# Weight tiles loaded through ScalarE's queue, and softmax weights turned on VectorE and through DRAM instead of on TensorE

## The chip, the cores and the metric

The kernel runs on one core of one Trainium2 chip. The metric is the device time of the whole program in microseconds (us), as a median over several executions. One execution was taken with the hardware profiler; every time that is read from a profile belongs to that execution.

Five engines work side by side: TensorE (PE in the profile, with its weight loads as PEld), VectorE (DVE), ScalarE (ACT), GpSimd (POOL) and SyncE (SP), which here only issues transfers. A transfer (DMA) is issued from the instruction stream of one engine and then runs by itself.

## The reference

One step of a decoder layer for a prompt of 1024 tokens and, with the same weights, for a sample group of 8 sequences of one token. One combined projection of the normalised input feeds three branches: gated linear attention (GLA), multi-scale pooling, and attention to 256 memory tokens ("cross"). Cut to what matters here:

```
h = rmsnorm(x, norm_gain)
proj = h @ w_in                          # 1024 x 10256
q, k, v, gla_g, a_lr, u, pool_g, xq, xg, merge = split(proj)
...
def cross_attn(q, mk, mv):               # 4 heads of 256, 256 memory tokens
    s = einsum('bthd,bmhd->bhtm', q, mk) * (XA_HEAD_DIM ** -0.5)
    p = softmax(s, axis=-1)
    return einsum('bhtm,bmhd->bthd', p, mv)
c = cross_attn(xq, mem_k, mem_v)         # the sample rows have a memory of their own, one per sequence
br_x = c * silu(xg)
...
merged = sum(sigmoid(merge) * (branches @ w_branch))
y = rmsnorm(x + merged @ w_out)
```

All of it is fp32.

## The kernel before

**Precision.** A large product is made of three: each operand is split into a high part (a copy in TensorE's fast fp32r type, on ScalarE) and a low part (the rest, by a subtraction on VectorE). `split`, `split_r`, `split_in` do that, `mm3` is the three matmuls (lines 242 to 244: high x high, high x low, low x high).

**The input projection** runs as 40 `Pair`s, each of 256 columns of `w_in`. `load` brings the weights of a pair as two halves of 512 KB ("raw", a pool of three buffers). A pair is computed by seven products instead of eight (a Strassen-Winograd scheme), whose left operands are a11, a12, s2, s1, s3, s4 and a22, made of quarters of the raw tiles and their sums (`operands`). `seq` is the list of all products in order, `prepare` makes operands up to three products ahead of TensorE, and `run_product` runs one: 24 matmuls for each of two halves of the columns (one half of 258 columns per `yield`). In `prepare` stand the raw loads too: the high half of pair i+1 at product 4 of pair i, the low half of pair i+2 at product 6 of pair i. Both are issued by SyncE.

**Everything else is filled in between.** The cross stage, then GLA, then pooling are written as generators that yield after each small step, and `fill` runs such steps between the halves of products, according to a budget of work. So TensorE's and SyncE's instruction order is that in which the code is written (`manual_schedule`); on VectorE, ScalarE and GpSimd a scheduler of the language sets the order.

**The cross stage** (`cross_steps`, some 119 to 380 us) goes through 16 units, a unit being one of four heads and one of four chunks of 256 tokens. For a unit: `cross_fetch` and `cross_queries` load and split the queries; `cross_scores` makes scores (12 matmuls), the maximum, the exponential and the scaled softmax weights `p`, with tokens on the partitions; `cross_weights` turns `p` (four transposes on TensorE into one bank of PSUM) and splits it to `pT`, with memory positions on the partitions; `cross_values` multiplies `pT` with the memory's values (12 matmuls), copies the result out and writes it to DRAM. Step s of the loop does scores of unit s, values of unit s-2 and weights of unit s-1.

Between them runs a second chain, `cross_sample`, once for each head, for the sample rows, whose memory is another one for each sequence: `cross_rows` turns the eight queries and GpSimd writes them to DRAM (`xqs`); SyncE loads them back, two at a time and spread over all partitions (`qb`), with two blocks of keys (`kc`), in four rounds; VectorE multiplies and sums (L777); TensorE turns the sums `sc` (L791), then the softmax weights `ps` (L803), then multiplies with the values `vc` (L817). The tiles `kc`, `qb` and `vc` share a pool of four buffers (`V`).

Most other tiles of the stage (`xq`, its high part, `p`, `pT`, its parts, `xo`) come from one ring of 14 buffers (`R`, NR). PSUM has six banks for the projection (`PX`) and two for the stage (`PZ`).

GLA already has the detour that the change uses: `gla_out` transposes in blocks of 32 x 32 on VectorE (`go`, L992) and sends the blocks to their places in DRAM by four transfers on GpSimd (`onsc`, L994).

Of the kernel before, what the change touches and what calls it, by code (L numbers as in the profile page):

```python
# [18 lines left out]
P = 128  # L19
# [5 lines left out]
NH = 4  # L25
# [8 lines left out]
CT = 256  # L34
# [13 lines left out]
def trunk_kernel(ctx: ExitStack, tc: tile.TileContext,  # L48
# [3 lines left out]
    nc = tc.nc  # L52
# [46 lines left out]
    def PZ():  # L99
        return ps.tile([P, 512], F32, tag="pz", name="pz", bufs=2)  # L100
# [36 lines left out]
    ident = cp.tile([P, P], F32, name="ident")  # L137
# [67 lines left out]
    xq_scr, v_scr = scratch(NH, "xqs", (NS, 256)), scratch(NH, "vs", (NS, 256))  # L205
    acc_scr = [scratch(NK, f"acc{n}_", (P, TT)) for n in range(2)]
    mkv_scr = [scratch(NH, f"mkvs{o}", (P, 2, DV)) for o in range(2)]
    al_scr = scratch(2, "als", (P, HT))
# [9 lines left out]
    last = {}  # L218
# [10 lines left out]
    def split_r(src, shape, name, scale=None):  # L229
        hi, lo = R(shape, F32R, name + "h"), R(shape, F32R, name + "l")  # L230
        split(hi, lo, src, scale)
        return hi, lo

    def split_in(x, shape, name, scale=None):

        hi, lo = R(shape, F32R, name + "h"), x.bitcast(F32R)
        split(hi, lo, x, scale)
        return hi, lo

    def mm3(out, lh, ll, rh, rl, start, stop, more=False):  # L240

        nc.tensor.matmul(out, lhsT=lh, rhs=rh, start=start, stop=False, skip_group_check=more)  # L242
        nc.tensor.matmul(out, lhsT=lh, rhs=rl, start=False, stop=False, skip_group_check=more)  # L243
        nc.tensor.matmul(out, lhsT=ll, rhs=rh, start=False, stop=stop, skip_group_check=more)  # L244
# [42 lines left out]
    class Pair:  # L287
# [3 lines left out]
            self.src, self.dst, self.s0, self.gated, self.raw = src, dst, s0, gated, [None, None]  # L291
            self.turned = turned

        def load(self, i):
            raw = RAW("raw")
            nc.sync.dma_start(out=raw, in_=self.src.rearrange("(k p) n -> p k n", p=P)[:, 4 * i:4 * i + 4])
            self.raw[i] = raw

        def operands(self):
# [26 lines left out]
    pairs = []  # L326
# [8 lines left out]
    NPAIR = len(pairs)  # L335
# [12 lines left out]
    def prepare(n):  # L348

        while prep["n"] < min(n + 1, len(seq)):  # L350
            i, j = seq[prep["n"]]
            p = pairs[i]
            if j == 0:
                p.gen = p.operands()
            left[i, j] = next(p.gen)

            if (i, j) == (0, 1):
                pairs[1].load(0)
            if j == 4 and i + 1 < NPAIR:
                pairs[i + 1].load(1)  # L360
            elif j == 6 and i + 2 < NPAIR:
                pairs[i + 2].load(0)
            prep["n"] += 1


# [334 lines left out]
    def cross_scores(h, c):  # L700
        xh, xl = cross["q", h, c]
        mh, ml = cross["mk", h]
        t = PZ()
        for j in range(2):
            for i in range(2):
                cs = slice(j * P, (j + 1) * P)
                mm3(t[:, j * NM:(j + 1) * NM], xh[:, i, cs], xl[:, i, cs], mh[:, i], ml[:, i], i == 0, i == 1)
        nm = tiny(2, "nm")
        nc.vector.tensor_reduce(nm, t.rearrange("p (j m) -> p j m", j=2), axis=AX.X, op=ALU.max, negate=True)
        p = R([2, NM], name="p")  # L710
        sm = tiny(2, "sm")
        for j in range(2):
            act(p[:, j], t[:, j * NM:(j + 1) * NM], AF.Exp, bias=nm[:, j:j + 1], accum_out=sm[:, j:j + 1])
        nc.vector.reciprocal(sm, sm)
        for j in range(2):
            nc.vector.tensor_scalar(p[:, j], p[:, j], sm[:, j:j + 1], None, op0=ALU.mult)
        cross["p", h, c] = p

    def cross_weights(h, c):
        p = cross["p", h, c]  # L720
        t = PZ()
        for a in range(2):
            for j in range(2):
                nc.tensor.transpose(t[:, (2 * a + j) * P:(2 * a + j + 1) * P], p[:, j, a * P:(a + 1) * P], ident)
        cross["pT", h, c] = split_r(t.rearrange("p (a t) -> p a t", a=2), [2, CT], "pT")

    def cross_values(h, c):
        ph, pl_ = cross["pT", h, c]
        vh, vl = cross["mv", h]
        g = R([2, CT], name="xo")  # L730
        t = PZ()
        for i in range(2):
            cs = slice(i * P, (i + 1) * P)
            for a in range(2):
                mm3(t[:, i * CT:(i + 1) * CT], vh[:, a, cs], vl[:, a, cs], ph[:, a], pl_[:, a], a == 0, a == 1)
        nc.scalar.activation(g, t.rearrange("p (i t) -> p i t", i=2), AF.Copy)
        nc.gpsimd.dma_start(out=mix_chunk(2, h, c), in_=g)

# [93 lines left out]
    def cross_steps():  # L832
        def scores(n):
            cross_scores(n // 4, n % 4)

        def memory(n):
            if n % 4 == 0:
                cross_memory(n // 4)

        def weights(n):  # L840
            cross_weights(n // 4, n % 4)

        def values(n):
            cross_values(n // 4, n % 4)

        samples = chain_of(cross_sample(h) for h in range(NH))
        cross_load(0)
        cross_memory(0)
        cross_fetch(0, 0)
        yield 2  # L850
        cross_queries(0, 0)
        cross_fetch(0, 1)
        for s in range(16 + 2):
            if s < 16:
                scores(s)
                yield 3
                if s + 1 < 16:
                    cross_queries(*divmod(s + 1, 4))
                if s + 2 < 16:
                    cross_fetch(*divmod(s + 2, 4))  # L860
            if s % 4 == 2 and s < 14:
                cross_load(s // 4 + 1)
            if s >= 1:
                yield next(samples, 0)
            if 0 <= s - 2:
                values(s - 2)
                yield 1.7
# [404 lines left out]
    for tb in range(4):  # L1272
        load_x(tb)
    next(memory)
    pairs[0].load(0)
    for tb in range(4, 8):
        load_x(tb)
    pairs[0].load(1)

    mem_transposed()  # L1280
    next(memory)
# [196 lines left out]
    for hf, order in enumerate(ORDERS):  # L1478
        for tb in order:
# [23 lines left out]
            n, a = hf, 0  # L1503
# [62 lines left out]
```

## Time and profile before

| | |
|---|---|
| median of 3 executions | 1443.5 us (1441.85 to 1443.95) |
| the profiled execution | 1445.01 us, of which the span of instructions 1443.3 |
| TensorE's granted clock, mean | 0.997 |
| busy: PE / DVE / ACT / POOL | 98% / 63% / 47% / 15% |
| moved by transfers | 259.42 MB, 180 GB/s |

How to read it: "busy" is the share of the span in which an engine executed instructions. A row of waits names the engine and line that waited, and behind `<-` the engine, the tile and the line that ended last before it could go on. Matmuls are pipelined, so a matmul's own duration (0.28 us) is longer than the distance between two starts (0.12 us); the distance is what it costs. In names of operations, `pz<-ident,p` is: out, then in. Line numbers are those of the kernel before; behind the change the same code stands one to six lines lower.

### The profile page before, as it was taken

The page shows a single profiled execution, that of the slowest core. Times are in us where ns is not written, and L with a number is a line of the kernel's source. Part 1 is how long each engine was busy: PE and PEld are TensorE (multiplying, and loading weights), DVE is VectorE, ACT ScalarE, POOL GpSimd, SP SyncE. Part 2 cuts the span into 40 slices and gives each one's busy share as a digit, 9 for nine tenths or more (in the row PEclk, how much of TensorE's full clock was granted, in tenths as well). Part 3 has the DMA queues.
Part 4 walks back from the last instruction along what each step waited for, and adds up shares of the span by engine and source line. Part 5 has one row for each costly group of instructions (what it writes and reads, how often), then busy time and mean ns, then how long its engine had stood idle before and what let it go on. Part 6 is the DMA issues. An engine that isn't in the chain of part 4 may idle for free.

```text
span 1443.3 us, 28179 instructions
## 1 busy us (share of the span) xinstructions
PE 1417.4 (98%) x10689; PEld 1356.1 (94%) x10689; DVE 916.2 (63%) x2123; ACT 679.0 (47%) x1575; POOL 222.1 (15%) x401
## 2 busy tenths in 40 slices
PE   8999999999999999999999999999999999999998
PEld 6899999989899999999999999999999999999876
DVE  6954756666687777767766778785672434554436
ACT  6743544443465666656654445444472432233212
POOL 3211111124342121212221111111010000000000
PEclk9999999999999999999999999999999999999999
DMA  9355665656656363554654455454694777632633
GB/s 329 125 165 169 217 218 187 207 175 165 198 155 193 115 192 129 182 176 126 187 167 150 149 188 170 159 184 163 204 298 134 234 257 249 234 104 79 224 118 116
DMA packets 183507, 259.42 MB, mean 180 GB/s; under 512 B 22204, under 2 KB 132564, under 8 KB 183364
## 3 DMA queue, kind: packets, MB, share of 16 engines
q1 hardware_dynamic: 159900, 183.87, 41.5%
q0 software_dynamic: 23328, 73.56, 14.7%
q8 instruction: 84, 1.38, 0.4%
q14 instruction: 51, 0.42, 0.1%
q10 hardware_dynamic: 144, 0.20, 0.0%
HBM read 180.47 MB, written 77.56 MB: 179 GB/s over the span
## 4 chain that ended last, share of the span: by engine, by line
PE 88%; DMA 5%; DVE 5%; issue 1%; ACT 1%; SPq 0%; POOL 0%; DVEq 0%; ACTq 0%; POOLq 0%
PE px L242 25%; PE px L243 25%; PE px L244 25%; DMA qb<-xqs 3%; PE pz L244 2%; PE pz L243 2%; PE pz L242 2%; DMA raw<-in_w_in_dram 1%; DVE kc L777 1%; PE pz L963 1%; PE pz L404 1%; PE pz L944 1%; PE pz L817 1%; PE pz L946 1%; PE pz L907 0%
## 5 line engine op out<-in xcount | busy, mean ns | idle before, releaser
L244 PE MATMUL px<-bh,wbl 128*128 128x384 f32 (+1 forms) x576 | 184.1, 320 | 0.0
L243 PE MATMUL px<-bl,wbh 128*128 128x384 f32 (+1 forms) x576 | 184.1, 320 | 0.0
L242 PE MATMUL px<-bh,wbh 128*128 128x384 f32 (+1 forms) x576 | 183.7, 319 | 0.0
L554 ACT ACTIVATE r<-px 128x258 f32<-128x258 f32 x240 | 89.9, 375 | 47.4 <-PE px L244 46.9
L242 PEld LDWEIGHTS px<-bh,wbh 128*128 128x128 f32 x576 | 108.3, 188 | 0.0
L243 PEld LDWEIGHTS px<-bl,wbh 128*128 128x128 f32 x576 | 108.2, 188 | 0.0
L244 PEld LDWEIGHTS px<-bh,wbl 128*128 128x128 f32 x576 | 108.2, 188 | 0.0
L242 PE MATMUL px<-ot,s1h 128*128 128x258 f32 x320 | 94.1, 294 | 0.0
L242 PE MATMUL px<-o,a12h 128*128 128x258 f32 x320 | 93.4, 292 | 0.0
L242 PE MATMUL px<-ot,s3h 128*128 128x258 f32 x320 | 93.2, 291 | 0.0
L242 PE MATMUL px<-o,s4h 128*128 128x258 f32 x320 | 93.0, 291 | 0.2 <-DVE c L636 0.2
L242 PE MATMUL px<-o,a11h 128*128 128x258 f32 x320 | 92.8, 290 | 0.0
L242 PE MATMUL px<-ot,a22h 128*128 128x258 f32 x320 | 92.6, 289 | 0.0
L242 PE MATMUL px<-ot,s2h 128*128 128x258 f32 x320 | 92.2, 288 | 0.0
L243 PE MATMUL px<-o,a11h 128*128 128x258 f32 x320 | 91.1, 285 | 0.3 <-DVE o L224 0.3
L243 PE MATMUL px<-o,a12h 128*128 128x258 f32 x320 | 91.1, 285 | 0.0
L244 PE MATMUL px<-o,a12l 128*128 128x258 f32 x320 | 91.0, 284 | 0.0
L244 PE MATMUL px<-ot,s1l 128*128 128x258 f32 x320 | 90.9, 284 | 0.0
L243 PE MATMUL px<-ot,s1h 128*128 128x258 f32 x320 | 90.8, 284 | 0.0
L244 PE MATMUL px<-o,a11l 128*128 128x258 f32 x320 | 90.6, 283 | 0.0
L243 PE MATMUL px<-ot,s2h 128*128 128x258 f32 x320 | 90.1, 281 | 0.5 <-DVE ot L224 0.5
L243 PE MATMUL px<-ot,a22h 128*128 128x258 f32 x320 | 90.5, 283 | 0.0
(471 smaller groups left out, 4634.3 us busy)
## 6 DMA issues: line engine op xcount, KB each, us to landing
raw<-in_w_in_dram SPq DMA_DIRECT2D x80, 512.0 KB, 4.0
msc<-c POOLq DMA_DIRECT2D x24, 516.0 KB, 4.8
brsc<-c POOLq DMA_DIRECT2D x24, 516.0 KB, 3.7
sig<-msc SPq DMA_DIRECT2D x24, 516.0 KB, 6.0
brr<-brsc SPq DMA_DIRECT2D x48, 256.0 KB, 5.2
wbr<-in_w_branch_dram SPq DMA_DIRECT2D x24, 512.0 KB, 5.5
acc<-sig POOLq DMA_DIRECT2D x16, 516.0 KB, 5.2
acc<-acc SPq DMA_DIRECT2D x16, 516.0 KB, 7.0
```

The source lines that it names most:

```text
L242: nc.tensor.matmul(out, lhsT=lh, rhs=rh, start=start, stop=False, skip_group_check=more)
L243: nc.tensor.matmul(out, lhsT=lh, rhs=rl, start=False, stop=False, skip_group_check=more)
L244: nc.tensor.matmul(out, lhsT=ll, rhs=rh, start=False, stop=stop, skip_group_check=more)
L404: nc.tensor.matmul(t[:, :DV], lhsT=memT[k // 2][:, k % 2, a * P:(a + 1) * P], rhs=raw[k // 2][:, k % 2], start=k == 0, stop=k == NK - 1)
L554: nc.scalar.activation(r, acc[c][:, :QT], AF.Copy)
L777: nc.vector.tensor_tensor_reduce(kc[:, a, :], kc[:, a, :], qb[:, bb, :], scale=1.0, scalar=0.0, op0=ALU.mult, op1=ALU.add, accum_out=sc[:, ...
L817: nc.tensor.matmul(t[32 * j:32 * j + 32, :DV], lhsT=pm[:, a, 4 * i + j, :], rhs=vc[j][:, a, :], start=a == 0, stop=a == 1)
L944: nc.tensor.matmul(t[0:64, 0:P], lhsT=ki[:, 0:64], rhs=qi, start=True, stop=True)
L946: nc.tensor.transpose(t[:, P:2 * P], kt, ident)
L963: nc.tensor.matmul(to, lhsT=kiqi[:, 1, cs], rhs=st, start=False, stop=True)
```

## The change

Three things change.

1. `Pair.load` issues from ScalarE's instruction stream, behind the split that was recorded last (`issue_after(last["hi"])`). The first three loads stay with SyncE. The low half of a pair is now asked for at product 1 of the pair before, one product later than it was.
2. `p` is no longer turned on TensorE. VectorE transposes it in blocks of 32 x 32 (`pt`), four transfers on GpSimd write the blocks to their places in a new scratch in DRAM, SyncE loads the turned tile (`cross_turned`), and `cross_weights` splits it, the low part in place. Columns stand there in the order (q, j, c) and not (j, q, c), so `cross_values` reads and writes through views that put them right.
3. Weights and values of a unit come one step of the loop later: in step s values of unit s-3, and the load and split of unit s-2. The loop has one more step.

```
-        def load(self, i):
+        def load(self, i, queue=None):
             raw = RAW("raw")
-            nc.sync.dma_start(out=raw, in_=...)
+            (queue or nc.scalar).dma_start(out=raw, in_=...)
...
             if (i, j) == (0, 1):
-                pairs[1].load(0)
-            if j == 4 and i + 1 < NPAIR:
-                pairs[i + 1].load(1)
-            elif j == 6 and i + 2 < NPAIR:
-                pairs[i + 2].load(0)
+                pairs[1].load(0, nc.sync)
+            with tc.issue_after(last["hi"].ins):
+                if j == 4 and i + 1 < NPAIR:
+                    pairs[i + 1].load(1)
+                elif j == 1 and 0 < i < NPAIR - 1:
+                    pairs[i + 1].load(0)
...
-        cross["p", h, c] = p
+        pt = R([512], name="pt")
+        nc.vector.transpose(pt.rearrange("p (b j c) -> p j b c", j=2, c=32), p.rearrange("p j (b c) -> p j b c", c=32))
+        for q in range(4):
+            nc.gpsimd.dma_start(out=pt_scr[4 * h + c][:, :, q, :].rearrange("b r x -> r b x"),
+                                in_=pt[32 * q:32 * q + 32].rearrange("r (b x) -> r b x", b=8))

     def cross_weights(h, c):
-        p = cross["p", h, c]
-        t = PZ()
-        for a in range(2):
-            for j in range(2):
-                nc.tensor.transpose(t[:, (2 * a + j) * P:(2 * a + j + 1) * P], p[:, j, a * P:(a + 1) * P], ident)
-        cross["pT", h, c] = split_r(t.rearrange("p (a t) -> p a t", a=2), [2, CT], "pT")
+        cross["pT", h, c] = split_in(cross["pr", h, c], [2, CT], "pT")
+
+    def cross_turned(h, c):
+        cross["pr", h, c] = loaded(pt_scr[4 * h + c].rearrange("(a b) r q x -> (b r) a (q x)", a=2), [2, CT], "pT")

     def cross_values(h, c):
...
-                mm3(t[:, i * CT:(i + 1) * CT], vh[:, a, cs], vl[:, a, cs], ph[:, a], pl_[:, a], a == 0, a == 1)
+                rh, rl = (x[:, a].rearrange("p (q j c) -> p j q c", q=4, j=2) for x in (ph, pl_))
+                mm3(t[:, i * CT:(i + 1) * CT].rearrange("p (j q c) -> p j q c", j=2, q=4), vh[:, a, cs], vl[:, a, cs],
+                    rh, rl, a == 0, a == 1)
...
-        for s in range(16 + 2):
+        for s in range(16 + 3):
...
+            if 0 <= s - 2 < 16:
+                cross_turned(*divmod(s - 2, 4))
...
-            if 0 <= s - 2:
-                values(s - 2)
+            if 0 <= s - 3:
+                values(s - 3)
...
-            if 0 <= s - 1 < 16:
-                weights(s - 1)
+            if 0 <= s - 2 < 16:
+                weights(s - 2)
```

What stands where in the instruction streams is shown at two places. The first is GpSimd's stream at the start of the cross stage, before the change (`smp` and `xqsc` are copies and writes of the projection, `xqs` is the write of the sample queries of head 0):

```order
L593 DMA xqsc_171<-c_1175 128x2x516
L569 COPY smp<-c_1427 128x8
L593 DMA xqsc_171<-c_1427 128x1032
L752 DMA xqs_124<-qn 8x256
L569 COPY smp<-c_1541 128x2x4
L593 DMA xqsc_172<-c_1541 128x2x516
```

The same stretch of GpSimd's stream after the change (`pts` is the new scratch, one for each unit):

```order
L595 DMA xqsc_187<-c_1191 128x2x516
L571 COPY smp<-c_1443 128x8
L595 DMA xqsc_187<-c_1443 128x1032
L722 DMA pts_132<-pt 32x8x64 x4
L722 DMA pts_133<-pt 32x8x64 x4
L758 DMA xqs_124<-qn 8x256
L722 DMA pts_134<-pt 32x8x64 x4
L571 COPY smp<-c_1563 128x2x4
L595 DMA xqsc_188<-c_1563 128x2x516
```

The eight writes of the first two units now stand ahead of the write of the sample queries.

The second is ScalarE's stream at the first scores, before (`mkTh` and `mvsh` are splits of the memory's keys and values, `c` a copy out of PSUM, L75 the exponential):

```order
L223 ACTIVATE mkTh<-pz 128x512
L223 ACTIVATE mvsh<-mkv 128x512
L223 ACTIVATE s3h<-ws 128x512
L655 ACTIVATE c_1427<-px 128x258
L226 ACTIVATE xqsh<-xq 128x512
L75 ACTIVATE p,sm<-pz,nm 128x256 x2
```

And after:

```order
L224 ACTIVATE mkTh<-pz 128x512
L224 ACTIVATE mvsh<-mkv 128x512
L224 ACTIVATE s3h<-ws 128x512
L657 ACTIVATE c_1443<-px 128x258
L297 DMA raw<-in_w_in_dram 128x4x256
L227 ACTIVATE xqsh<-xq 128x512
L75 ACTIVATE p,sm<-pz,nm 128x256 x2
```

A raw load now stands between the split of s3, behind which it was written, and the split of the first queries.

More of the change, by code (lines that the diff above doesn't have):

```diff
@@ L205, in trunk_kernel @@
     xq_scr, v_scr = scratch(NH, "xqs", (NS, 256)), scratch(NH, "vs", (NS, 256))
+    pt_scr = scratch(4 * NH, "pts", (8, 32, 4, 64))
     acc_scr = [scratch(NK, f"acc{n}_", (P, TT)) for n in range(2)]
@@ L292, in __init__ @@
             self.turned = turned
-        def load(self, i):
+        def load(self, i, queue=None):
             raw = RAW("raw")
-            nc.sync.dma_start(out=raw, in_=self.src.rearrange("(k p) n -> p k n", p=P)[:, 4 * i:4 * i + 4])
+            (queue or nc.scalar).dma_start(out=raw, in_=self.src.rearrange("(k p) n -> p k n", p=P)[:, 4 * i:4 * i + 4])
             self.raw[i] = raw
@@ L1274, in trunk_kernel @@
     next(memory)
-    pairs[0].load(0)
+    pairs[0].load(0, nc.sync)
     for tb in range(4, 8):
         load_x(tb)
-    pairs[0].load(1)
+    pairs[0].load(1, nc.sync)
     mem_transposed()
```

## The prediction, on record before the changed kernel was run

> **What bounds the kernel.** I read the page first (engine shares, then the chain), then the same engines in four stretches, then TensorE's waits in the stretch that the change touches.
>
> ```profile
> span 1443.3 us, 28179 instructions
> PE 1417.4 (98%) x10689; PEld 1356.1 (94%) x10689; DVE 916.2 (63%) x2123; ACT 679.0 (47%) x1575; POOL 222.1 (15%) x401
> PE 88%; DMA 5%; DVE 5%; issue 1%; ACT 1%; SPq 0%; POOL 0%; DVEq 0%; ACTq 0%; POOLq 0%
> ```
>
> TensorE is busy for 98% of the span and is 88% of the chain. So only three things change the time: instructions that leave TensorE's stream, TensorE's idle time, and the clock that it is granted. The stretches show where it is idle (columns: us; then busy time and instructions of PE, PEld, DVE, ACT and POOL; granted clock; DMA share; GB/s):
>
> ```profile
> 119.00:200.00 81.00, 77.47 (x638) 74.46 (x637) 50.22 (x124) 36.40 (x90) 8.99 (x16) 0.98 0.56 172
> 200.00:300.00 100.00, 99.04 (x841) 97.06 (x840) 66.27 (x179) 46.05 (x112) 12.34 (x24) 1.00 0.65 208
> 300.00:380.00 80.00, 74.05 (x627) 69.85 (x626) 46.33 (x117) 30.34 (x72) 28.79 (x47) 0.98 0.65 187
> 380.00:1064.00 684.00, 683.35 (x5648) 665.90 (x5647) 502.37 (x1216) 379.00 (x957) 128.84 (x216) 1.00 0.54 168
> 125.00:135.00 10.00, 9.12 (x65) 8.87 (x65) 5.99 (x14) 4.37 (x13) 0.00 (x0) 0.85 0.32 106
> ```
>
> The cross stage runs from 119 to 380 us. There TensorE is idle for 3.5 + 1.0 + 5.9 = 10.4 us; from 380 to 1064, where weight loads go on, for 0.65 us. The last row shows that an idle spell costs more than itself: after one of about 1.4 us the clock over ten microseconds is 0.85, so about 1.5 us more go. The waits in that stage (us in total, times, longest):
>
> ```profile
> PE pz L803 <- DVE ps L798: 2.4, 1, 2.4
> PE pz L243 <- DVE pTl L224: 1.5, 1, 1.5
> PE pz L242 <- ACT xqsh L226: 1.4, 1, 1.4
> PE pz L724 <- ACT xo L736: 1.1, 1, 1.1
> PE pz L817 <- DVE pm L804: 1.0, 1, 1.0
> PE pz L791 <- DVE mkTl L224: 1.0, 1, 1.0
> PE pz L242 <- DVE pTl L224: 1.0, 1, 1.0
> ```
>
> L803, L817 and L791 belong to the eight sample rows' chain; the pT and xo waits stand at the softmax weights.
>
> **The change, part by part.**
>
> *Transposes out: -7.0 us.* Sixteen groups of four leave TensorE. Ahead of one group and behind it run the same products:
>
> ```profile
> 136.00 0.28 PE L244 MATMUL px<-ot,s1l 128*128 128x258 f32 x1
> 136.13 0.60 PE L724 MATMUL pz<-ident,p 128*128 128x128 f32 x4
> 136.48 0.37 PE L242 MATMUL px<-ot,s1h 128*128 128x258 f32 x1
> 136.68 0.28 PE L243 MATMUL px<-ot,s1h 128*128 128x258 f32 x1
> 136.80 0.28 PE L244 MATMUL px<-ot,s1l 128*128 128x258 f32 x1
> ```
>
> From the group's start to the second product behind it is 0.55 us; a product takes 0.12 (136.68 to 136.80). That leaves 0.43; 16 x 0.44 is 7.0 us, all on the bounding engine.
>
> *Waits tied to them: -3.6 us.* pTl 1.5 and 1.0, and xo 1.1 (L724 waited for a PSUM bank) lose their instruction or get a step more of time. 10.4 us were idle, so this is a third of it.
>
> *The way through DRAM: 0.* Per unit there is now a VectorE transpose, four GpSimd issues, a load by SyncE and a split. The gated-attention part does the same thing with the same shapes:
>
> ```profile
> L992 DVE STREAM_TRANSPOSE go<-on x16: 702/705/715, 421.2 to 745.0; 128x512 f32<-128x512 f32 x16
> L994 POOL DMA_DIRECT2D onsc<-go x64: 582/585/629, 423.9 to 747.7; - x64
> xq<-xqsc SPq DMA_DIRECT2D x14, 256.0 KB, 4.3
> qb<-xqs SPq DMA_DIRECT2D x16, 256.0 KB, 4.5
> ```
>
> VectorE gets 16 x 0.705 = 11.3 us, GpSimd 64 x 0.585 = 37 us, in 261 us where the rows above have VectorE busy for 163 and GpSimd for 50. The cover is TensorE's own order: between the scores behind which the load of the turned weights can go and the values that read them stand at least 109 matmuls, 133 at the first unit, 109 x 0.12 = 13 us. Against that stand 4.5 us of load and two splits of about 0.7. Without the cover each unit would cost up to the rest of that chain; some 7 us are spare, so I take zero; the end below nothing is already in the waits, the other end is 2 us for the first unit, whose writes come behind other work on GpSimd.
>
> *Values a step later, strided operand: 0.* The values' matmuls now read runs of 32 floats instead of 256 in a row. Their pace now is 0.115 us:
>
> ```profile
> 356.50 0.27 PE L242 MATMUL pz<-pTh,mvsh 128*128 128x256 f32 x1
> 356.61 0.28 PE L243 MATMUL pz<-pTl,mvsh 128*128 128x256 f32 x1
> 14.38 3.72 PE L404 MATMUL pz<-wm,memT 128*128 128x256 f32 x16
> ```
>
> No row shows such a reading. The upper bound is a matmul of plain fp32 at the same size, 3.72 / 16 = 0.23, so +0.115 x 192 = +22 us; below nothing there is no reason for a gain. I take zero, since the instructions, the element count and the type are those of the near row. The Trainium skill, page "PSUM — Partial Sum Buffer", section "Specifications (TRN2)", speaks against the change here: it says a non-contiguous access pattern slows matmuls significantly, and gives 8-byte lines. The new view of the output visits addresses that still run on, and the operand's runs fill whole lines; so by its reason the price is zero, by its wording up to that bound. No run so far shows which.
>
> *Weight loads on ScalarE's queue: +0.4 us.* 77 of the 80 loads of a raw half move from SyncE to ScalarE.
>
> ```profile
> L296 SPq DMA_DIRECT2D raw<-in_w_in_dram x80: 367/383/1928, 11.0 to 1032.6; - x80
> raw<-in_w_in_dram SPq DMA_DIRECT2D x80, 512.0 KB, 4.0
> SPq L296 <- DVE a22l L224: 160.3, 20, 12.6
> SPq L296 <- DVE ws L305: 144.0, 20, 10.4
> 168.02 0.68 DVE L224 TENSOR_TENSOR a22l<-raw,a22h 128x512 fp32r<-128x512 f32 x1
> 168.32 0.63 ACT L223 ACTIVATE a12h<-raw 128x512 fp32r<-128x512 f32 x1 [0.26 <-PE px L243]
> ```
>
> ScalarE issues 77 x 0.38 = 29 us more, at 47% load. A load stands behind the split that its product issues (L223), and the slot that it overwrites is free once VectorE has read it. The low half is now asked for one product later, behind a12h; the last reader of its slot, a22l of the pair before, ended at 168.70, a12h at 168.95, and this pair is the tightest of 38. So ScalarE waits for nothing. From there to its first use four products of 24 matmuls run by the order (96 x 0.12 = 11.5 us), against 4.0 us of landing, so that TensorE doesn't notice. The one place where it counts is the stage's start, where a load (0.38) now stands right ahead of xqsh, for which TensorE waits already. Between 0 and 0.8 us.
>
> SyncE is freed: it stood for 160.3 + 144.0 us at these loads with whatever was queued behind them. TensorE's waits name none of its loads, and the Trainium skill, page "DMA: Bandwidth & Descriptors", section "Issuing engines are not separate DMA queues", says that several issuing engines save issue time only; that agrees with a gain of nothing by itself. What it can unblock is the sample chain:
>
> *The sample chain: +5.0 us (+6.0 - 1.0).* Its links for head 0 are these:
>
> ```profile
> 136.07 0.53 POOL L752 DMA_DIRECT2D xqs<-qn  x1 [13.06 <-ACT qn L751]
> 139.51 0.34 SPq L767 DMA_DIRECT2D qb<-xqs  x1
> 144.02 0.43 DVE L777 CUSTOM_DVE_ANT_0 kc<-kc,qb 128x256 f32<-128x256 f32 x1 [3.52 <-DMA qb<-xqs]
> 166.35 0.42 DVE L777 CUSTOM_DVE_ANT_0 kc<-kc,qb 128x256 f32<-128x256 f32 x1
> 169.36 0.38 PE L791 MATMUL pz<-ident,sc 128*8 128x128 f32 x2 [0.97 <-DVE mkTl L224]
> DVE kc L777 <- DMA qb<-xqs: 24.2, 11, 4.1
> ```
>
> The row of sums is ready at 166.8; TensorE would have come to L791 at 169.36 - 0.97 = 168.4, so 1.6 us were spare. After the change less lies ahead of L791: by the order, 24 fewer products (24 x 0.12 = 2.9), three groups of transposes (1.3) and twelve values (1.4), 5.6 us in all. And the xqs write on GpSimd stands behind eight of the new writes (8 x 0.585 = 4.7, of which about 2 come at a time when it had been idle for 13 us and only then hold it up). The chain through four rounds has no spare of its own: four V buffers, each round asked for once the last is read, VectorE waiting for qb eleven times. So L791 waits 5.6 - 1.6 + (0 to 2) = 4 to 6 us, less up to 1 if SyncE, freed of raw loads, comes sooner: 3 to 6, I take 4.5, and 1.5 for the clock after it. The 0.97 of before is contained. Bounds 0 (the rounds get faster by SyncE's freedom) and 8.
>
> In heads 1 to 3 TensorE comes earlier too, but SyncE no longer stands at raw loads ahead of their kc loads. I set these against each other: 0, between -4 (the 2.4 and 1.0 at L803 and L817 go) and +9 (three waits of 3 us).
>
> **The sum.** -7.0 - 3.6 + 0 + 0 + 0.4 + 6.0 - 1.0 = -5.2 us. The profiled execution took 1445.0 us (span 1443.3 and 1.7 around it), 1.5 above the median of 1443.5; off the median that gives 1438.3.
>
> **The rivals.**
> 1. *SyncE's freedom is worth more than TensorE's haste*, and the sample chain causes no wait: -7.0 - 3.6 - 1.0 - 2.4 - 1.0 and about 1.7 of clock = -16.7 at most; 1430 with some of it lost. For it: 304 us of SyncE at two lines. Against: the qb waits show rounds bound by landing and buffers. 0.20.
> 2. *The sample chain takes it all back.* Heads 1 to 3 wait for 2 to 3.5 us each: no change (1441 to 1446), 0.19. At over 3.5 a head it is slower, which is the rival on the other side: 6 + 9 - 11.2 = +3.8, 1447; 0.08. For it: the same number of steps is taken out ahead of every head's L791.
> 3. *ScalarE is held at its load issues* by a slot or a completion counter that it shares with SyncE's loads, and with it the copies out of PSUM. The row pair at 168 has only 0.25 us between the two ends. It decides from 5.2 / 77 = 0.07 us an issue on; at 0.11, all paid by TensorE, 1447; 0.05.
> 4. *The strided operand is slow:* 1438.3 + 22 = 1460; 0.05. It decides from 5.2 / 192 = 0.027 us a matmul on. For it: nothing in the rows; against it: the count and type of elements are unchanged. (This is where the wording of the Trainium skill's page "PSUM — Partial Sum Buffer" leads.)
>
> That leaves 0.43 for the forecast, whose own range is 1434 to 1441.
>
> **How the numbers follow.** The runs of before lie 2 us apart; 0.2%, 2.9 us, is what can be told from no change. Faster: 0.43 + 0.20 = 0.63. Same: 0.19. Slower: 0.08 + 0.05 + 0.05 = 0.18. Range 1429 to 1448: it takes in rivals 1 to 3 and leaves out the strided case and the ends of 1 and 2.
>
> **What the profile after would show.** No matmul with the identity at the softmax weights, and PE's busy time about 7 us less; values' matmuls still 0.115 apart (or else rival 4); no wait of TensorE named pTl; a wait at the first sc transposes of 3 to 6 us with kc or sc as its releaser (0 under rival 1, and one in each head under rival 2); raw loads under ACTq with no time between the split and the issue (rival 3 otherwise). From 380 us on nothing should move. I am wrong if the sample chain's rounds (144.0 to 166.8 in head 0) get shorter, or if the load of turned weights comes late in every unit.

## The result and the profile after

The changed kernel took 1468.2 us (median of 4, 1465.2 to 1470.8), the kernel before 1443.7 (median of 4 on the same chip): the ratio is 1.0176, with a 95% interval of 1.0159 to 1.0193. The forecast was 1438.3, with a range to 1448. So it was wrong by its sign, and by 30 us. The two profiled executions lie 20.1 us apart where the medians lie 24.5: the kernel after was caught in the fastest of its four, the kernel before 1.3 us above its median.

The page of the kernel after, where it answers to the lines of before:

```profile
span 1463.4 us, 28256 instructions
...
PE 1418.4 (97%) x10625; PEld 1354.5 (93%) x10625; DVE 925.8 (63%) x2139; ACT 679.2 (46%) x1575; POOL 257.5 (18%) x465
...
PE 78%; DMA 4%; DVE 3%; issue 2%; ACT 1%; SPq 1%; POOL 0%; DVEq 0%; ACTq 0%
```

64 matmuls fewer, 64 GpSimd issues more, all as written; and yet the span is 20.1 us longer. Only GpSimd is fuller, by three points of its share. To see where the time went, I took the same products of the projection in both traces (TensorE's order of products is the same in both) and cut the span at the fifth, the fifteenth, the 80th and the 101st. (A product is 24 matmuls in all, 12 for each half of its columns.) From the fifteenth on to the 80th is the cross stage; from the 80th to the 101st is the gated attention's beginning; up to the fifth is the start. The columns are those of the windows shown with the prediction. Before:

```profile
0.00:69.60 69.60, 61.42 (x390) 51.37 (x391) 53.90 (x103) 47.36 (x93) 18.70 (x51) 1.00 0.70 233
117.70:390.60 272.90, 262.46 (x2199) 253.16 (x2198) 172.53 (x445) 120.64 (x291) 53.09 (x92) 0.99 0.62 190
390.60:466.90 76.30, 75.64 (x618) 71.95 (x618) 61.06 (x156) 47.00 (x129) 29.64 (x49) 1.00 0.60 169
```

After:

```profile
0.00:74.30 74.30, 62.93 (x389) 52.89 (x390) 54.32 (x103) 47.35 (x92) 18.68 (x51) 0.95 0.66 219
122.40:404.60 282.20, 261.31 (x2135) 249.91 (x2134) 181.21 (x462) 120.02 (x291) 89.68 (x156) 0.98 0.70 213
404.60:487.10 82.50, 76.74 (x618) 72.18 (x617) 61.62 (x157) 46.78 (x129) 29.00 (x50) 1.00 0.56 161
```

The start is 4.7 us longer, the cross stage 9.3 (with 64 matmuls fewer), the attention's beginning 6.2. That is the whole difference of the two spans: 20.2 of 20.1. In the cross stage TensorE's idle time went from 10.4 to 20.9 us. From there to the end the two traces run 20.2 us apart, to within 0.1. TensorE's waits in the kernel after (us in total, times, longest):

```profile
PE pz L797 <- DVE sc L783: 10.6, 3, 4.0
...
PE px L496 <- DVE h L506: 3.9, 1, 3.9
PE px L243 <- DVE c L638: 3.5, 3, 2.0
PE px L243 <- DVE c L621: 3.2, 1, 3.2
...
PE pz L823 <- ACT r L556: 1.8, 1, 1.8
...
PE pz L244 <- DVE pT L225: 0.8, 1, 0.8
```

Three places, three kinds. L797 is the sample rows' sums, in heads 0, 1 and 3. L496 at the start waits for `h`, a row of VectorE's that the change doesn't touch. L638 and L621 are adds of the projection on VectorE: TensorE waits for a PSUM bank that such an add must first read. At pT, where the new way through DRAM ends, it waits for 0.8 us in all: from TensorE that way is hidden, as forecast. ScalarE, which splits the turned tile, stood 17.4 us for it, in six waits.

### The profile page after: what moved, and what is told of

It is laid out like the page before. It is cut to its first block, busy times and chain, and to the rows that moved or that the text cites. A ratio compares the mean times of both kernels' runs of the same rounds, so it can differ in the third digit from the quotient of the medians.

```text
span 1463.4 us, 28256 instructions
## 1 busy us (share of the span) xinstructions
PE 1418.4 (97%) x10625; PEld 1354.5 (93%) x10625; DVE 925.8 (63%) x2139; ACT 679.2 (46%) x1575; POOL 257.5 (18%) x465
## 4 chain that ended last, share of the span: by engine, by line
PE 78%; DMA 4%; DVE 3%; issue 2%; ACT 1%; SPq 1%; POOL 0%; DVEq 0%; ACTq 0%
PE px L243 23%; PE px L244 23%; PE px L245 23%; DMA qb<-xqs 3%; PE pz L243 2%; PE pz L244 2%; PE pz L245 2%; DVE kc L783 1%; DMA vc<-in_cache_mem_v_dram 1%; PE pz L971 1%; PE pz L952 1%; PE pz L823 1%; SPq L672 1%; PE pz L954 1%; PE pz L915 0%
## 5 line engine op out<-in xcount | busy, mean ns | idle before, releaser
L243 PE MATMUL px<-ot,s3h 128*128 128x258 f32 x320 | 93.5, 292 | 0.0
L243 PE MATMUL px<-ot,s1h 128*128 128x258 f32 x320 | 93.1, 291 | 0.0
L243 PE MATMUL px<-ot,s2h 128*128 128x258 f32 x320 | 92.4, 289 | 0.0
L245 PE MATMUL px<-ot,s3l 128*128 128x258 f32 x320 | 90.8, 284 | 0.0
L244 PE MATMUL px<-ot,s3h 128*128 128x258 f32 x320 | 90.6, 283 | 0.0
L245 PE MATMUL px<-o,s4l 128*128 128x258 f32 x320 | 90.6, 283 | 0.0
```

## The experiments

The first column of numbers is the median of the run, the second the median of the kernel before on the same chip, the interval that of the ratio. The last three are the lengths of the three stretches in each run's profile, cut at the same products. Each length is that of one execution, and executions of one version of the changed kernel lie up to 7.9 us apart. So a few us between two versions that have the turn are not told apart by a length.

| run | us | before | ratio, 95% | start | cross | attention |
|---|---|---|---|---|---|---|
| before | | | | 69.6 | 272.9 | 76.3 |
| after | 1468.2 | 1443.7 | 1.0159 to 1.0193 | 74.3 | 282.2 | 82.5 |
| 1 turn without queue | 1471.5 | 1443.5 | 1.0186 to 1.0226 | 69.2 | 288.4 | 86.9 |
| 2 queue alone | 1449.1 | 1443.5 | 1.0032 to 1.0062 | 75.3 | 271.7 | 76.4 |
| 3 queue warmed | 1466.6 | 1443.5 | 1.0141 to 1.0192 | 71.9 | 280.7 | 85.0 |
| 4 later step alone | 1457.4 | 1443.5 | 1.0064 to 1.0118 | 69.6 | 284.6 | 76.3 |
| 5 before, no samples | 1417.3 | 1441.7 | 0.9818 to 0.9847 | 70.0 | 247.2 | 76.4 |
| 6 after, no samples | 1432.6 | 1441.7 | 0.9923 to 0.9955 | 74.4 | 239.7 | 90.3 |
| 7 sums later | 1459.2 | 1441.7 | 1.0093 to 1.0136 | 75.2 | 279.8 | 83.3 |
| 8 later step, no samples | 1418.6 | 1441.7 | 0.9824 to 0.9853 | 69.8 | 245.8 | 76.3 |
| 9 six buffers | 1497.2 | 1443.9 | 1.0343 to 1.0393 | 73.2 | 288.1 | 84.2 |
| 10 order held | 1469.4 | 1443.9 | 1.0161 to 1.0210 | 73.4 | 287.8 | 86.2 |
| 11 three mended | 1496.9 | 1443.9 | 1.0349 to 1.0408 | 68.7 | 290.7 | 86.4 |
| 12 before, six buffers | 1487.3 | 1443.9 | 1.0270 to 1.0327 | 69.0 | 277.8 | 82.9 |
| 13 writes on ScalarE | 1472.7 | 1442.1 | 1.0196 to 1.0231 | 74.3 | 294.5 | 76.5 |
| 14 turn, not later | 1463.6 | 1442.1 | 1.0132 to 1.0165 | 73.1 | 283.8 | 83.0 |
| 15 mended | 1468.5 | 1442.1 | 1.0164 to 1.0198 | 69.2 | 294.1 | 76.5 |
| 16 queries off SyncE | 1475.9 | 1442.1 | 1.0215 to 1.0264 | 73.9 | 297.6 | 84.0 |
| 17 queue alone, mended | 1444.0 | 1442.6 | 1.0003 to 1.0021 | 69.6 | 273.4 | 76.4 |
| 18 best try | 1470.3 | 1442.6 | 1.0171 to 1.0203 | 69.8 | 299.4 | 75.9 |

### One part at a time

**Run 1**, the loads back on SyncE:

```
-            (queue or nc.scalar).dma_start(out=raw, ...)
+            (queue or nc.sync).dma_start(out=raw, ...)
```

(and in `prepare` the two loads at products 4 and 6, as before the change).

> The change with the weight loads back on SyncE in their old places; only the turn through DRAM and the later step are left. Theory A (the first load on ScalarE's queue costs the 5 us at the start, the rest of the loss is the sample chain and VectorE's order in the cross stage, which the turn causes): about 5 us less than the changed kernel, 1463. Theory B (the queue move is the cause, in the stage too, since loads come later and VectorE stands behind them): 1443.7 - 7 = 1437.

Neither: it is no faster than the changed kernel (1471.5 against 1468.2). The start is mended, 69.2, but the cross stage lost 6.2 us more and the attention 4.4 more. By these single profiles the queue move costs the start and pays for it in the two stretches behind. The medians, 3.5 us apart when each is set against the kernel before on its own chip, agree with that.

**Run 2**, the queue move alone.

> The kernel before with only the queue move (and the low half asked for a product later). Theory A: 1443.7 + 5 = 1449, all of it before 70 us. Theory B: 1443.7 + 24.5 + 7 = 1475, since the turn would then be a gain of 7. In between, 1455 to 1465: both parts lose on their own.

1449.1, as theory A had it: +5.6; in the profile 5.7 lie before the fifth product, and the cross stage is 1.2 shorter. Theory B falls.

**Run 3**, a 2 KB load on ScalarE's queue at the very beginning:

```
-        nc.gpsimd.dma_start(out=rows[n:...], in_=src...)
+        (nc.scalar if n == 24 else nc.gpsimd).dma_start(out=rows[n:...], in_=src...)
```

> The changed kernel, with the load of one small vector (2 KB) moved from GpSimd's to ScalarE's queue at the very start, so that the first load there is not that of a weight half. Theory A: the first issue's 4.0 us fall where ScalarE has nothing to do, and the 5 us at the start go: 1463. Rival: the 4.0 us and the late landing belong to the load's place or its slot and not to the queue's first use: 1468.

Half of it. These rows of the kernel after show the start's loss: ScalarE's first load issue took 4.00 us, and stopped ScalarE for 2.89; VectorE stood at a row that needs the load, and `h`, for which TensorE waits, stands behind it.

```profile
37.45 4.00 ACTq L297 DMA_DIRECT2D raw<-in_w_in_dram  x1
...
41.50 1.15 ACT L480 ACTIVATE x<-x,rr 128x1024 f32<-128x1024 f32 x1 [2.89 <-issue]
...
47.18 0.69 DVE L306 TENSOR_TENSOR ws<-raw 128x512 f32<-128x512 f32 x1 [3.29 <-DMA raw<-in_w_in_dram]
47.79 0.68 DVE L506 TENSOR_TENSOR h<-px,vec 128x512 f32<-128x512 f32 x1
```

With the small load first:

```profile
37.59 0.42 ACTq L297 DMA_DIRECT2D raw<-in_w_in_dram  x1
...
46.26 0.69 DVE L306 TENSOR_TENSOR ws<-raw 128x512 f32<-128x512 f32 x1 [4.97 <-DMA raw<-in_w_in_dram]
46.87 0.68 DVE L506 TENSOR_TENSOR h<-px,vec 128x512 f32<-128x512 f32 x1
```

The issue takes 0.42, and the start is 2.4 us shorter; but VectorE still stands at `ws`, now for 4.97 us, because there `ws` is ordered ahead of `h`. The small load's own issue took 0.57 us: the 3.6 us were not moved to a harmless place, they are gone, and why a first load there is slow when it is a large one isn't shown. In the kernel before, `ws` stood behind `h`:

```profile
43.93 0.69 DVE L504 TENSOR_TENSOR h<-px,vec 128x512 f32<-128x512 f32 x1 [2.20 <-PE px L494]
...
44.80 0.69 DVE L504 TENSOR_TENSOR h<-px,vec 128x512 f32<-128x512 f32 x1
...
45.48 0.68 DVE L305 TENSOR_TENSOR ws<-raw 128x512 f32<-128x512 f32 x1
```

**Run 17** puts the second pair's first load back on SyncE as well:

```
-                    pairs[i + 1].load(1)
+                    pairs[i + 1].load(1, nc.sync if i == 0 else None)
```

> The queue move alone (as in the second run), with the first load of the second pair back on SyncE and ScalarE's queue first used by a 2 KB load. If the queue's whole loss is the start: 1449.1 - 5 = 1444, the kernel before within 2 us; its cross stage was 1.2 us shorter, so 1442 at best. Rival (77 issues on ScalarE cost something everywhere): 1447 or more.

1444.0 against 1442.6; the start is 69.6 as before. The queue move loses 5.6 us by its start and little else: 1.0003 to 1.0021 is what is left.

**Run 4**, the later step alone, with the turn still on TensorE (the three changed lines of the loop in `cross_steps`, without `cross_turned`).

> The kernel before with weights and values one step of the loop later, still turned on TensorE, weight loads on SyncE. Theory A: the transposes stay and the sample chain has nothing new before it, though TensorE's other waits at pT and xo go (3.6 us) and twelve values fewer stand ahead of the first sums (up to 1.5 more wait): 1441 to 1444. Rival (the later step is what makes TensorE come too early for the sample chain): a wait in each head, 1450 or more.

The rival: +13.9 by the medians; in the profile 11.7 lie in the cross stage. In the code nothing but the place of weights and values in the loop had moved. Its waits, the sample chain's in the main:

```profile
PE pz L817 <- DVE pm L804: 3.4, 2, 2.6
PE pz L791 <- DVE mkTl L224: 3.1, 1, 3.1
PE pz L242 <- DVE pTl L224: 3.0, 1, 3.0
PE pz L817 <- DMA vc<-in_cache_mem_v_dram: 1.5, 3, 0.7
...
PE pz L749 <- DVE mkTl L224: 1.3, 1, 1.3
```

### Without the sample chain

Runs 5, 6 and 8 leave out all that `cross_sample` issues (its steps of planned work stay, its result is zero).

> The kernel before without the sample rows' chain of the cross stage (their keys, scores, softmax and values are left out; their result is zero; the steps of work that it was planned with stay). It is the base for the next two: its 160 matmuls take some 12 us, its waits 5: about 1426.

> The changed kernel without the sample rows' chain. Theory S (what the change costs in the cross stage is the sample chain, which it leaves no time): against the kernel before without that chain it is 7 us of transposes faster, 5 us at the start and up to 6 in the gated attention slower: a difference of 0 to +5. Rival (the turn itself, its load on VectorE, SyncE and the ring of tiles is the cause): a difference of +15 to +25.

> The kernel with the later step alone, without the sample rows' chain. Theory S: no difference from the kernel before without that chain, within 3 us. Rival (the ring of 14 tiles, which the later step holds longer): most of the 12 to 14 us stay.

The cross stage of the kernel before without the chain, then of the kernel after without it, then of the later step alone without it:

```profile
118.10:365.30 247.20, 244.71 (x2030) 243.97 (x2029) 148.10 (x290) 115.52 (x271) 50.76 (x88) 0.99 0.42 124
```

```profile
122.50:362.20 239.70, 236.28 (x1966) 235.35 (x1965) 156.74 (x303) 114.49 (x269) 87.98 (x152) 1.00 0.57 162
362.20:452.50 90.30, 80.00 (x619) 75.23 (x619) 63.06 (x160) 48.13 (x131) 29.33 (x50) 0.94 0.55 150
```

```profile
117.90:363.70 245.80, 243.17 (x2031) 242.44 (x2030) 147.76 (x290) 115.62 (x271) 50.47 (x88) 1.00 0.43 125
```

This is the main finding. With no sample chain the change makes the cross stage 7.5 us shorter, the price of the transposes, and the later step costs nothing (-1.4). With the chain the same change makes it 9.3 longer, and the later step alone 11.7. So all of the stage's loss, 9.3 + 7.5 = 16.8 us, comes by way of the sample chain: it lengthens the stage by 25.7 us in the kernel before and by 42.5 in the kernel after. The whole of run 6 came out at +15.3 against run 5, where I had expected at most +5. In the profiles it is +12.8: the start +4.4, the cross stage -7.5, the attention +13.9 (the second row of run 6) and +2.0 behind it.

**Run 7** moves 1.2 units of planned work from the chain's end to the place ahead of the sums.

```
             yield 1
-        yield 0.5
+        yield 1.7
+        yield 0
         t = PZ()
```

(and the chain's last `yield 1.2` becomes `yield 0`).

> The changed kernel with the sample rows' sums turned a little later in each head (1.2 units of the planned work moved from the chain's end to before it): TensorE then reaches them 12, 72, 48 and 24 matmuls later (1.4, 8.6, 5.8 and 2.9 us). Theory S: the waits of 4.0, 3.5 and 3.2 us there shrink to 2.6, 0 and 0.3, with their clock some 10 us: 1458. Rival: the waits come back at the chain's next links, 1466 to 1470.

1459.2: by the medians 9.0 less than the changed kernel, or 7.0 with each set against the kernel before on its own chip. That is the forecast number, but not its mechanism: of the three waits at the sums only head 1's went, head 0's is 3.9 and head 3's 4.8 us. The profile can't show what was gained, since it caught the slowest of the four executions (1464.5).

**Runs 9, 11 and 12**: six buffers for the chain, at the price of one of 30 large tiles; run 11 with the order held (below) and the start mended too.

> The changed kernel with six instead of four buffers for the sample rows' keys, queries and values (and 29 instead of 30 large tiles, for the room): each round's loads can go before the products of the round ahead. Theory S (the chain's rounds, each load waiting for the last round's reads, set TensorE's waits): the chain of four rounds gets up to 3 x 4 us shorter and the 10.6 us of waits at the sums go, with some clock: 1453 to 1457. Rival (the chain is held by VectorE's and SyncE's order, not by its buffers): 1465 or more.

> The changed kernel with all three: six sample buffers, the order held, and at the start the first weight load of the second pair on SyncE as before (and ScalarE's queue first used by a 2 KB load). If the three causes are apart and all that there is, 1468 - 12 - 6 - 5 = 1445; with the 7 us that the turn saves it ends below the kernel before only if the chain's other links (values, softmax) wait no more either.

> The kernel before with six sample buffers and 29 large tiles. Its chain had 1.6 us spare at the first sums and waits of 2.4 and 1.0 at its later links: at most 5 us with the clock, 1439 to 1443; slower only if the missing large tile is needed, which would then also weigh on the two runs above.

As totals these tell nothing: the two edits together cost the kernel before 43 us. In run 9 TensorE waited at the sums 0.6 us in head 0, 0.3 in head 1 and not at all in head 3, instead of 4.0, 3.5 and 3.2. But that isn't shown to be the buffers' doing. Counted from the stage's start, the sums were ready no sooner in head 0 (51.4 us against 50.4), and 1.6 and 3.3 us sooner in heads 1 and 3; for the rest TensorE came later, by new waits of its own (4.2 us at the first queries). In run 11 the start was mended (68.7), and it is no faster than run 9.

**Run 16** takes the queries' loads off SyncE.

```
-        cross["xq", h, c] = loaded(chunk_of(xq_raw[h], c), [2, CT], "xq")
+        x = cross["xq", h, c] = R([2, CT], name="xq")
+        (nc.gpsimd if c + h else nc.sync).dma_start(out=x, in_=chunk_of(xq_raw[h], c))
```

> The changed kernel with the loads of the queries (xq) issued by GpSimd instead of SyncE. Theory Q (SyncE stands at these loads until the ring of 14 tiles has a free one, seven tiles a step being taken now, and the sample chain's loads stand behind: 202 to 214 us in head 1): the waits at the sums of heads 1 and 3 go, 1460. Rival (SyncE's standing there is not what the chain waits for): 1468.

Not as theory Q had it: the stage got 15 us longer, and the sums still waited (2.4, 3.0 and 3.6 us). But this run doesn't settle the theory, for SyncE did not come free: the turned tiles' loads and those of the memory still stood in its stream, and its waits that ended at a transpose `pt` on VectorE came to 49.8 us, where the changed kernel has 37.0.

```profile
SPq L672 <- DVE pt L721: 49.8, 7, 15.0
```

**Run 14** undoes the later step and keeps the turn (`cross_turned` and `cross_weights` for unit s-1, `cross_values` for s-2).

> The changed kernel without the later step: the turned weights are loaded and split in the step after the scores, values two steps after, as before. Theory S (the later step takes work out from ahead of the sample chain's links; by the order TensorE now reaches the first sums 3 instead of 39 rows earlier than before): the cross stage gets back most of the 12 us that the later step cost alone, 1452 to 1456. Rival (the later step is needed to hide the way through DRAM): TensorE waits at pT in each unit, 16 x 1 us or more, 1470 and up.

Neither. Head 0 is mended: its sums wait 0.7 us, and the seven products around them take 28.7 us as before (34.0 after the change). TensorE has no wait at pT, so the way through DRAM doesn't need the later step on TensorE's account; ScalarE stood 13.9 us for the turned tiles. But TensorE then waits in head 1 at the sample values (3.2 in three waits), and in heads 2 and 3 at an add (3.1), at the values (1.7), at the sums (3.0) and at the softmax (3.5), and the stage is as long as that of the changed kernel (283.8).

### The gated attention

**Run 10** holds the attention's work on VectorE behind the projection's add that was written ahead of it, up to 490 us (the add is kept in `last["c"]`):

```
+                if gla and slot < 210:
+                    with tc.issue_after(last["c"].ins):
+                        cost = next(self.steps, None)
```

> The changed kernel with VectorE's order held in the first part of the gated attention (to 490 us): what a step of it issues on VectorE stands behind the projection's add that was written ahead of it. Theory O (the 6 us between 400 and 480 us are VectorE's order: the add for which TensorE waits stands behind the attention's work): the wait of 3.2 us at 472 and those of 0.8 to 0.9 go, 1462. Rival (the attention's inputs come late, by transfers): no change, 1468.

The wait at 472 us went, and one of 4.4 at the attention's own gate (L915) came in its place; the stretch is 86.2. Holding one piece of the order moves the loss.

**Run 13** issues the 64 new writes from ScalarE.

```
-            nc.gpsimd.dma_start(out=pt_scr[4 * h + c]...
+            nc.scalar.dma_start(out=pt_scr[4 * h + c]...
```

> The changed kernel with the writes of the turned weights issued by ScalarE instead of GpSimd. In the order of instructions this alone puts VectorE's work of the gated attention back among the projection's adds as it stood before. Theory G (the planner reckons GpSimd's 64 more issues as late inputs of the gated attention, and orders VectorE by that): the 6 us between 400 and 480 go: 1462, less or more by what 64 x 0.37 us on ScalarE cost in the cross stage. Rival (the attention's loss has another cause, the order is innocent): 1468 or more, with the waits at the attention's lines still there.

Its attention stretch:

```profile
416.90:493.40 76.50, 75.89 (x619) 72.06 (x618) 61.15 (x157) 46.94 (x129) 29.06 (x50) 1.00 0.63 178
```

76.5 against 76.3 before and 82.5 after: theory G's part. GpSimd's own busy time there is 29 to 30 us in all three. What differs is VectorE's order: here the adds (c) stand among the attention's rows as they did before, and in the changed kernel they were behind them. The changed kernel, with TensorE's wait:

```profile
465.07 0.48 DVE L899 TENSOR_SCALAR bz<-pz,vec 128x256 f32<-128x256 f32 x1 [0.80 <-ACT bz L898]
...
471.53 0.75 DVE L621 TENSOR_TENSOR c<-px,r 128x258 f32<-128x258 f32 x2
472.00 0.39 PE L243 MATMUL px<-o,a11h 128*128 128x258 f32 x1 [3.16 <-DVE c L621]
```

Run 13:

```profile
471.39 0.75 DVE L621 TENSOR_TENSOR c<-px,r 128x258 f32<-128x258 f32 x2
...
474.73 0.48 DVE L899 TENSOR_SCALAR bz<-pz,vec 128x256 f32<-128x256 f32 x1 [1.19 <-ACT bz L898]
```

That the planner counts GpSimd's issues as late inputs is my reading of it; that 64 writes on another engine's queue put these adds and the time back is shown. The writes on GpSimd are not the only condition, for in run 18 (below) GpSimd writes too. The stage got 12 us longer with the writes on ScalarE, which stood in waits that ended with them:

```profile
ACT xo L742 <- DMA pts<-pt: 18.9, 4, 7.9
...
ACT r L556 <- DMA pts<-pt: 9.5, 2, 4.8
```

**Runs 15 and 18** put together what had mended single places: 15 is 13 and 14 with the start mended, 18 is 14 with the start mended and run 7's shift, in which VectorE's adds stand among the attention's rows again with GpSimd writing.

> Both of these, and the start mended (first load of the second pair on SyncE, ScalarE's queue first used by a 2 KB load). If start (5), attention (6) and later step (12) are the whole loss, what is left is the 7 us of transposes and the end's 3: 1468 - 5 - 6 - 14 = 1443 at worst, 1437 at best; the first version that may beat the kernel before.

> The turn through DRAM without the later step, start mended, the sums of the sample chain moved later as in the seventh run, and GpSimd writing (in the order of instructions VectorE's work in the gated attention stands as before). The start gives 5 and the attention 6 against the changed kernel; the cross stage lost 11 us against before in the fourteenth run, of which the sums' and softmax' waits of 3.0 and 3.5 us in head 3 should go: 1448 to 1453. Below 1443 only if VectorE's adds no longer come late in heads 2 and 3.

Start and attention are mended in both (69.2 and 76.5; 69.8 and 75.9), so these two causes stand alone and are removed. The cross stage isn't: 294.1 and 299.4. In run 18 the shift that had helped in run 7 gave a wait of 7.9 us at the sums of head 3. No version with the turn beat the kernel before.

## Why the prediction was wrong, by its steps

- *Transposes, -7.0.* Right: the stage without the chain is 7.5 us shorter (run 6 against run 5). (16 x 0.43 is 6.9.)
- *Waits tied to them, -3.6.* They went as named, but for 0.8 us at pT and 0.8 at an xo; what came in their place at other lines was not in the sum.
- *The way through DRAM, 0.* TensorE hardly sees its transfers (0.8 us of waits at pT). But the step looked for its cost on the path of the data, and costs were elsewhere. With 64 issues more on GpSimd the planner gave VectorE another order in the attention, some 100 us behind the last of them, which cost 6.2 (run 13 takes it back; so does run 18, with the issues still on GpSimd). "From 380 us on nothing should move" was wrong for this reason. And the new loads stand in SyncE's stream with those of the sample chain (below).
- *Strided operand, 0.* Right. The values' matmuls start 0.12 apart as before (0.119 on the mean in both kernels; the 0.115 of the prediction was read from two starts):

```profile
249.15 0.29 PE L244 MATMUL pz<-pT,mvsh 128*128 128x256 f32 x1
249.27 0.28 PE L245 MATMUL pz<-pTh,mkv 128*128 128x256 f32 x1
249.39 0.28 PE L243 MATMUL pz<-pTh,mvsh 128*128 128x256 f32 x1
```

  So the price of zero is right. It doesn't decide between the two readings of the Trainium skill's page "PSUM — Partial Sum Buffer", section "Specifications (TRN2)": that row is one on PSUM, where only the output lies, whose addresses run on. The operand in runs of 32 floats is a tile of the ring, not of PSUM. No run here has an output whose addresses don't run on.
- *Weight loads on ScalarE's queue, +0.4.* Mis-sized: +5. The issue at 0.38 was taken from SyncE's rows; the first one on ScalarE's queue took 4.00 us (run 3 shows 0.42 behind a small load). The rest is VectorE's order of `ws` and `h`: with that load on ScalarE `ws` stands ahead, also where the issue is short (run 3), and with it back on SyncE the rest of the loss went too (run 17). At the later issues ScalarE did wait for nothing, as forecast.
- *SyncE freed, 0.* Rival 1 had at most something in it: against run 1 the queue move takes 6.2 us from the stage, if the turn is there; if not, the stage is 1.2 shorter in run 2 and 0.5 longer in run 17.
- *The sample chain.* This is the step that failed. Head 0 went as forecast: counted from the stage's start, TensorE came to the sums 4.5 us sooner (46.2 against 50.7), the sums were ready 1.3 later (50.4 against 49.1), and it waited 4.0 us where 4.5 had been taken. Its rounds did get 2 us shorter, which the prediction had called a sign of being wrong, but they began 3.6 later. What failed is "in heads 1 to 3 ... I set these against each other: 0". TensorE's haste, on one side, is not what these heads show: with its earlier waits counted in, it came to the sums no sooner than before (115.6 against 114.2 us in head 1, 247.3 against 241.3 in head 3). SyncE's freedom, on the other side, was not there. The sums were ready 7.2 and 9.7 us later, and TensorE waited 3.5 and 3.2. So rival 2 ("the sample chain takes it all back") had waits of about the right size, in two of three heads, but not for its reason, that TensorE comes too soon in every head.

  Why the chain came later can be read from SyncE's rows. Where it no longer stands at a raw load, it stands at the next load whose tile isn't free, and the chain's loads stand behind. Its waits that ended at a transpose `pt` on VectorE (us in total, times, longest) are an example. The longest, 14.4 us, was between the two turned tiles' loads (`pT`) ahead of head 3's first keys:

```profile
SPq L672 <- DVE pt L720: 37.0, 7, 14.4
```

```profile
324.11 0.52 SPq L672 DMA_DIRECT2D xq<-xqsc  x1
327.17 15.19 SPq L672 DMA_DIRECT2D pT<-pts  x2
342.41 1.64 SPq L672 DMA_DIRECT2D kc<-in_cache_mem_k_dram  x2
```

  In the kernel before, the same keys were asked for 13.3 us sooner, counted from the stage's start:

```profile
323.90 0.37 SPq L296 DMA_DIRECT2D raw<-in_w_in_dram  x1
324.36 0.97 SPq L670 DMA_DIRECT2D kc<-in_cache_mem_k_dram  x2
```

  By the code a step now takes seven tiles of the ring of 14 where it took six. That this is why SyncE stands there is my reading; no run gave the ring more tiles or took the turned loads off SyncE.

  What no case held is that the chain also sits in VectorE's queue. Where VectorE stands at a `kc` row for its `qb`, the projection's adds ordered behind it come later:

```profile
300.11 0.42 DVE L783 CUSTOM_DVE_ANT_0 kc<-kc,qb 128x256 f32<-128x256 f32 x1 [1.26 <-DMA qb<-xqs]
...
301.50 0.69 DVE L225 TENSOR_TENSOR a22l<-raw,a22h 128x512 fp32r<-128x512 f32 x1
302.10 0.42 DVE L638 TENSOR_TENSOR c<-px,r 128x258 f32<-128x258 f32 x1
...
302.57 0.39 PE L243 MATMUL px<-o,s4h 128*128 128x258 f32 x1 [2.02 <-DVE c L638]
```

  Behind the waits of heads 0 and 1 the granted clock fell as well (0.88 from 172 to 186 us, 0.81 from 241 to 250), behind that of head 3 it didn't (1.00 from 372 to 376). In all the chain came to 16.8 us, where I had +6 - 1.
- The later step's 11.7 us (run 4) lie at links that I hardly asked about: only for the first sums of head 0 did I count what work no longer covers them.

**What stays open.** Within the stage's 16.8 us the single links weren't told apart: undoing the later step (run 14), more buffers (9), a later place of the sums (7, 18) and the queries' loads on GpSimd (16) each moved the waits to another link. How much of it is the turn's 16 x 0.7 us on VectorE, and how much the new loads that share SyncE with the chain's, no run says; the rows above show only that the second delays the chain. The waits under a wait of VectorE that I read from rows were not taken away by themselves.

## What to carry to other kernels

Where a second, tightly linked chain runs beside the main one, price a change by what it takes out from ahead of each of the chain's links, in every round of it, and by what it puts ahead of the chain's loads in the stream that issues them. An issuing engine that loses one load to wait at may only wait at the next. Leave the chain out in a run to see its share: here that one pair of runs turned the cross stage's loss of 9 us into the gain of 7 that was forecast. Instructions added to an idle engine may change the order that a planner gives another engine; compare the order far behind the change, too. And look at the first transfer on another queue by itself.

## What the hardware showed that I had not expected

The first transfer that ScalarE issued, a weight load, took 4.00 us of issue, against 0.37 for the median of its weight loads; in the nine kernels where it was the first it took 3.70 (run 2) to 5.11 (run 6). Behind an early 2 KB load, whose own issue took 0.57 us in run 3, the first weight load there took 0.41 to 0.42 in five kernels (runs 3, 11, 15, 17, 18). A moving operand in runs of 32 floats cost TensorE nothing (0.119 us a matmul before and after).
